# Final norm of the last token half: squares summed by a matrix of ones, the root by ScalarE and a Newton step on rows, other tiles for GpSimd

## The chip, the cores and the metric

The kernel runs on one core of a Trainium2 chip. The core has five engines that work beside each other, each through its own queue in order: TensorE (PE: matrix products; PEld is its loading of the stationary operand), VectorE (DVE), ScalarE (ACT), GpSimd (POOL) and SyncE (SP, which here only issues transfers). The metric is the device time of one execution in microseconds (us); less is better.

## What is computed

One layer of a hybrid decoder over 512 tokens of width 2048, and then a last RMSNorm. The change concerns only the last line:

```python
def rmsnorm(x, w):
    xf = x.astype(jnp.float32)
    y = xf * lax.rsqrt(jnp.mean(xf * xf, axis=-1, keepdims=True) + EPS)
    return (y * w.astype(jnp.float32)).astype(x.dtype)

...
        x = x + conv_ffn(rmsnorm(x, norm2_w[l]), ffn_up[l], ffn_conv_w[l], ffn_down[l])
    return rmsnorm(x, final_norm_w)
```

Each token's 2048 values are divided by the root of their mean square and multiplied by a weight for each of the 2048 features.

## The kernel before

**Layout.** Activations lie transposed: 128 features on the partitions, tokens along the row. The 2048 features are 16 tiles `acc[0]` to `acc[15]` of 128x512; two neighbours share a buffer `acc2[d // 2]`. In the profile the buffer appears as `accd`. Because features lie on partitions, a token's sum of squares runs over partitions and over the 16 tiles, and needs TensorE.

**The last stretch.** The down projection of the feed-forward part adds its products into `acc` chunk by chunk. The last chunk of both weight halves is treated apart, and in two token halves `t` = 0 and 1 of 256 tokens (`HS`), so that the norm of half 0 can run beside the products of half 1. For each tile `d` of a half (function `parts`): six products into a PSUM tile `ps_e` (L201 to L203: float32 values split into a high and a low part), VectorE adds it to `acc[d]` (L1089), ScalarE squares the result (L1095 for d = 0, straight into the running sum `s3`; L1097 into `sq` for the others), and GpSimd adds the square to `s3` (L1099). The last `NP[t]` squares (2 in half 0, 6 in half 1) aren't added by GpSimd but go to TensorE.

**The norm of a half** (generator `finish`, L1039 to L1056). ScalarE multiplies the tiles that GpSimd is to scale, d >= `ND_` = 10, by their norm weight (L1042, "prescale" below). TensorE then sums squares over the partitions (`sums`, L1034): each square is the stationary operand, in two pieces of 128 tokens, and a single column of ones is the moving one; so the sums stand as 128x2, token on partition. VectorE takes the mean and the inverse root by an integer guess and three Newton steps, twelve operations on 128x2 (L1048 and L130 to L135). TensorE turns the result back into a row of 256 tokens on all partitions, in PSUM (L118, tile `n_ps`), and ScalarE copies it to SBUF (L1055, `r3`; the profile calls it `rstd`).

**Scaling** (`scale`). For d < 10, VectorE multiplies `acc[d]` by the norm weight and by the row in PSUM (L1063). For the other six, GpSimd multiplies the prescaled tile by the copy `r3` (L1066). After each odd tile SP issues the transfer of the pair to the output `outT` (L1068).

**Order.** In this stretch the order on TensorE, SP, VectorE, ScalarE and GpSimd is that in which the program issues the instructions; a small clock `self.now`, moved by estimates, decides when a waiting generator such as `finish` goes on between products. The scaling of half 0 is issued between the tiles of half 1: behind tile d > `AFTER` = 9 of half 1 stand the scalings of tiles d - 10 and, on GpSimd, d. All tiles of half 1 are scaled at the end, after the last product.

Of the kernel before, what the change touches and what calls it, by code (L numbers as in the profile page):

```python
# [8 lines left out]
F32 = mybir.dt.float32  # L9
# [3 lines left out]
AF = mybir.ActivationFunctionType  # L13
ALU = mybir.AluOpType
# [4 lines left out]
P = 128  # L19
S = 512  # L20
D = 2048
KT = D // P
# [6 lines left out]
EPS = 1e-6  # L29
# [50 lines left out]
class Body:  # L80
# [704 lines left out]
    def out_phase(self):  # L785
        tc, nc, io = self.tc, self.nc, self.io
        with ExitStack() as ctx:
            pool = lambda name, **k: ctx.enter_context(tc.tile_pool(name=name, **k))
            g2 = pool("g2", bufs=1)
# [227 lines left out]
            j0 = NFF - G  # L1017
            wl = [wd[c - 1], wd[c]]
            HS = S // 2
            NP, ND_ = (2, 6), 10  # L1020
            s3 = g2.tile([P, 2, HS], F32, tag="ssum", name="ssum3")
            r3 = g2.tile([P, 2, HS], F32, tag="rstd", name="rstd3")

            pts, norm_row, sq4 = {}, {}, {}
            AFTER = 9

            def sums(t, parts, last=False):

                first = t not in pts
                if first:  # L1030
                    pts[t] = self.mm.tile([P, S], F32, tag="mm", name=f"ps_n3_{t}")
                for i, q in enumerate(parts):
                    for c in range(HS // P):
                        nc.tensor.matmul(pts[t][:, c:c + 1], q[:, c * P:(c + 1) * P], self.ones[:, 0:1],  # L1034
                                         start=first and i == 0 and c == 0, stop=last and i == len(parts) - 1,
                                         skip_group_check=True)
                        self.now += 0.21

            def finish(t, late):  # L1039
                sl = slice(t * HS, (t + 1) * HS)  # L1040
                for d in range(ND_, KT):
                    nc.scalar.activation(acc[d][:, sl], acc[d][:, sl], AF.Copy, scale=self.prm("nf", d))  # L1042
                yield 4.0 if t == 0 else 0.5
                n = HS // P
                sums(t, late[-2:] + [s3[:, t, :]], last=True)
                pt = pts[t]
# [8 lines left out]
                nc.scalar.copy(out=r3[:, t, :], in_=ps[:, 0:HS])  # L1055
                norm_row[t] = ps  # L1056

            def scale(t, e):

                sl = slice(t * HS, (t + 1) * HS)  # L1060
                a = acc[e][:, sl]
                if e < ND_:
                    nc.vector.scalar_tensor_tensor(out=a, in0=a, scalar=self.prm("nf", e), in1=norm_row[t][:, 0:HS],  # L1063
                                                   op0=ALU.mult, op1=ALU.mult)
                else:
                    nc.gpsimd.tensor_tensor(out=a, in0=a, in1=r3[:, t, :], op=ALU.mult)  # L1066
                if e % 2:
                    nc.sync.dma_start(out=io["outT"][:, e - 1:e + 1, sl], in_=acc2[e // 2][:, :, sl])  # L1068

            for t in range(2):  # L1070
                sl = slice(t * HS, (t + 1) * HS)
# [8 lines left out]
                def parts(ds):  # L1080
# [4 lines left out]
                    for d in ds:  # L1085
# [12 lines left out]
                        if d < KT - NP[t]:  # L1098
                            nc.gpsimd.tensor_tensor(out=s3[:, t, :], in0=s3[:, t, :], in1=q, op=ALU.add)  # L1099
                        else:  # L1100
                            late.append(q)
                            if len(late) > 2:
                                sums(t, late[-3:-2])
                        if t == 1 and d > AFTER:
                            self.ensure(lambda: 0 in norm_row)
                            scale(0, d - AFTER - 1)
                            if d - AFTER - 1 + ND_ < KT:
                                scale(0, d - AFTER - 1 + ND_)

                if n8:  # L1110
                    parts(range(n8))
                for d in range(n8, KT):
                    parts([d])
                if t == 1:
                    for e in range(KT - AFTER - 1, ND_):
                        scale(0, e)
                self.spawn(finish(t, late))
            self.ensure(lambda: not self.cos)
            for e in (0, 1, 10, 2, 3, 11, 4, 5, 12, 6, 7, 13, 8, 9, 14, 15):
                scale(1, e)  # L1120


class UpProjection:
# [191 lines left out]
```

## Time and profile before

| | |
|---|---|
| median of 3 runs | 2228.73 us (2227.31 to 2229.14) |
| profiled execution, its own time | 2227.93 us |
| its span in the trace | 2226.2 us |
| TensorE busy | 2198.1 us, 99% of the span |
| VectorE busy | 1519.4 us, 68% |
| ScalarE busy | 947.7 us, 43% |
| GpSimd busy | 426.1 us, 19% |
| granted TensorE clock, mean | 0.995 of full speed |

A row of the timeline gives start, duration, engine, line of the program, operation, output <- inputs, shape and count, and in brackets how long the engine had been idle before it and what ended that. Rows that are merged ("x5") overlap a little at their seams. Times are from the start of the span. A group of the costliest instructions shows busy time in us, mean duration in ns, and idle time before them.

### The profile page before, as it was taken

Reading aid. Unit: us, or ns where it says so; the run is one execution under the profiler, and the core shown is the slowest. Engines: PE = TensorE matmul, PEld = TensorE weight load, DVE = VectorE, ACT = ScalarE, POOL = GpSimd, SP = SyncE. Lnnn points to the kernel's source line nnn. Section 1 sums busy time; section 2 is a strip of 40 time slices with the busy share of each in tenths; the row PEclk is TensorE's granted clock in tenths of the full one; section 3 lists DMA queues with packets and bytes.
Section 4 is the critical chain, followed back from the end, with each engine's and each line's share of the span. In section 5 each row is a group of like instructions: output and inputs, shape, how many; then the busy total and the mean of one; then the engine's idle time right before and its main releaser. Section 6 shows DMA issues by size and latency. Waiting matters only on the chain.

```text
span 2226.2 us, 35449 instructions
## 1 busy us (share of the span) xinstructions
PE 2198.1 (99%) x13998; PEld 1990.0 (89%) x13998; DVE 1519.4 (68%) x2346; ACT 947.7 (43%) x1377; POOL 426.1 (19%) x519
## 2 busy tenths in 40 slices
PE   8999999999999999999999999999999999999997
PEld 6888888888888999999999999999998888888887
DVE  7766667665445776766676666677667777777776
ACT  6656455434334544444444444444443222222223
POOL 5270811800121211111111111111110000000004
PEclk9999999999999999999999999999999999999998
DMA  6232232323534788888888888888885333333342
GB/s 199 77 111 67 79 102 83 100 66 119 193 118 137 168 204 196 206 207 200 201 196 198 206 203 199 202 196 201 219 192 188 130 125 116 123 114 123 114 129 99
DMA packets 109207, 340.01 MB, mean 153 GB/s; under 512 B 12720, under 2 KB 19120, under 8 KB 109040
## 3 DMA queue, kind: packets, MB, share of 16 engines
q1 hardware_dynamic: 78576, 229.72, 30.2%
q0 software_dynamic: 30464, 108.02, 26.6%
q8 instruction: 110, 1.80, 0.3%
q14 instruction: 57, 0.47, 0.1%
HBM read 314.36 MB, written 23.33 MB: 152 GB/s over the span
## 4 chain that ended last, share of the span: by engine, by line
PE 90%; DVE 3%; POOL 3%; issue 2%; DMA 1%; ACT 1%; SPq 0%; POOLq 0%; ACTq 0%; DVEq 0%
PE ps_y L1193 18%; PE ps_x L1193 12%; PE ps_z L1193 12%; PE ps_d L203 8%; PE ps_d L201 7%; PE ps_d L202 7%; PE ps_u L201 4%; PE ps_u L202 4%; PE ps_u L203 4%; PE ps_o L202 3%; PE ps_o L201 3%; PE ps_o L203 3%; POOL tl L583 1%; POOL tm L581 1%; PE ps_x L118 1%
## 5 line engine op out<-in xcount | busy, mean ns | idle before, releaser
L1010 DVE TENSOR_TENSOR accd<-accd,ps_d 128x512 f32<-128x512 f32 x368 | 250.0, 685 | 125.3 <-PE ps_d L203 125.3
L201 PE MATMUL ps_d<-gh,whi_d 128*128 128x512 f32 x736 | 286.3, 389 | 0.0
L202 PE MATMUL ps_d<-gl,whi_d 128*128 128x512 f32 x736 | 286.3, 389 | 0.0
L203 PE MATMUL ps_d<-gh,wlo_d 128*128 128x512 f32 x736 | 286.3, 389 | 0.0
L1193 PE MATMUL ps_y<-fs,hi_t 128*128 128x256 f32 x1536 | 269.7, 278 | 2.6 <-ACT hi_b L1174 1.3
L274 ACT CAST whi_d<-raw_d 128x1024 fp32r<-128x1024 f32 x96 | 100.8, 1053 | 370.8 <-PE ps_d L202 346.9
L1175 DVE TENSOR_TENSOR lo_t<-ra,hi_t 128x1024 fp32r<-128x1024 f32 x144 | 176.0, 1223 | 114.3 <-ACT hi_t L1174 114.2
L201 PE MATMUL ps_u<-xh,hi_in 128*128 128x512 f32 x608 | 245.7, 404 | 0.0
L203 PE MATMUL ps_u<-xh,lo_in 128*128 128x512 f32 x608 | 237.9, 391 | 0.0
L202 PE MATMUL ps_u<-xl,hi_in 128*128 128x512 f32 x608 | 237.4, 391 | 0.0
L1193 PEld LDWEIGHTS ps_y<-fs,hi_t 128*128 128x128 f32 x1536 | 232.9, 188 | 3.0 <-ACT e L1215 1.5
L1178 POOL DMA_DIRECT2D ra<-in_w_up x144 | 126.2, 876 | 555.3 <-DVE lo_t L1175 455.9
L1193 PE MATMUL ps_y<-fs,lo_t 128*128 128x256 f32 x768 | 213.1, 277 | 0.0
L1174 ACT CAST hi_t<-ra 128x1024 fp32r<-128x1024 f32 x144 | 151.3, 1051 | 72.7 <-PE ps_y L1193 44.7
L202 PEld LDWEIGHTS ps_d<-gl,whi_d 128*128 128x128 f32 x736 | 138.2, 188 | 28.7
L203 PEld LDWEIGHTS ps_d<-gh,wlo_d 128*128 128x128 f32 x736 | 138.2, 188 | 28.6
L201 PEld LDWEIGHTS ps_d<-gh,whi_d 128*128 128x128 f32 x736 | 138.2, 188 | 28.5
L1193 PEld LDWEIGHTS ps_y<-fs,lo_t 128*128 128x128 f32 x768 | 144.4, 188 | 0.0
L1193 PE MATMUL ps_y<-fb,hi_t 128*128 128x256 f32 x768 | 140.1, 283 | 1.2 <-DVE e L1223 1.2
L1193 PE MATMUL ps_x<-fb,hi_b 128*128 128x256 f32 x768 | 140.1, 283 | 0.0
L1193 PE MATMUL ps_x<-fa,hi_b 128*128 128x256 f32 x768 | 140.0, 283 | 0.0
L203 PEld LDWEIGHTS ps_u<-xh,lo_in 128*128 128x128 f32 x608 | 114.2, 188 | 24.8
(357 smaller groups left out, 5087.8 us busy)
## 6 DMA issues: line engine op xcount, KB each, us to landing
ra<-in_w_up POOLq DMA_DIRECT2D x144, 512.0 KB, 7.8
raw_d<-in_w_down SPq DMA_DIRECT2D x96, 512.0 KB, 4.2
raw_in<-in_w_in SPq DMA_DIRECT2D x80, 512.0 KB, 3.7
ra<-in_w_up SPq DMA_DIRECT2D x48, 512.0 KB, 7.0
rc<-in_w_up SPq DMA_DIRECT2D x48, 512.0 KB, 6.6
rb<-in_w_up SPq DMA_DIRECT2D x48, 512.0 KB, 7.3
rb<-in_w_up POOLq DMA_DIRECT2D x48, 512.0 KB, 7.4
raw_o<-in_w_out SPq DMA_DIRECT2D x32, 512.0 KB, 3.7
```

The source lines that it names most:

```text
L118: self.nc.tensor.matmul(out, lhsT, rhs, start=True, stop=True)
L201: nc.tensor.matmul(ps, hi[:, sl], a, start=start, stop=False)
L202: nc.tensor.matmul(ps, hi[:, sl], b, start=False, stop=False)
L203: nc.tensor.matmul(ps, lo[:, sl], a, start=False, stop=stop)
L274: self.nc.scalar.copy(out=hi, in_=x)
L581: nc.gpsimd.tensor_tensor(out=t, in0=bc(ll[:, j, j + 1:32], j + 1), in1=tl[:, j:j + 1, 0:j + 1].broadcast_to([32, m, j + 1]), op=ALU.mult)
L583: nc.gpsimd.tensor_tensor(out=tl[:, j + 1:32, 0:j + 1], in0=tl[:, j + 1:32, 0:j + 1], in1=t, op=ALU.subtract)
L1010: nc.vector.tensor_tensor(out=acc[d], in0=acc[d], in1=ps, op=ALU.add)
L1174: nc.scalar.copy(out=hi, in_=raw)
L1175: nc.vector.tensor_tensor(out=lo, in0=raw, in1=hi.bitcast(F32), op=ALU.subtract)
L1178: nc.gpsimd.dma_start(out=raw, in_=self.block(j, self.NEXT[f]), accum_op=ALU.add)
L1193: mm = lambda w, x, s, e: nc.tensor.matmul(ps, w[:, sl], x, start=s, stop=e, skip_group_check=True)
```

## The change

For half 1, each square (and the running sum `s3`) is now the moving operand of one product with a 128x128 matrix of ones; the sum of a token then stands on all partitions at once, as a row of 256 tokens. ScalarE takes the square root of that row, and VectorE makes the inverse root by a reciprocal and one Newton step on 128x256; the result goes to `r3` in SBUF, and that is the row for both engines' scaling. Half 0 keeps the old way. The one use of the square root earlier, on a single value, stands where its table is loaded. GpSimd scales tiles 8 to 15 of half 0 and tiles 4 to 9 of half 1 (before: 10 to 15 of both); the prescales of half 1 stand behind the square of the same tile. Of half 1, tiles 0 and 1 are sent one by one.

```diff
-            NP, ND_ = (2, 6), 10
+            NP = (2, 6)
+            ON_POOL = range(8, 16), range(4, 10)
...
+            eps = g2.tile([P, 2], F32, name="eps")
+            nc.vector.memset(eps, EPS)
+            nc.scalar.activation(eps[:, 1:2], eps[:, 0:1], AF.Sqrt)
...
+                if t == 1:
+                    for i, q in enumerate(parts):
+                        nc.tensor.matmul(pts[t][:, 0:HS], self.ones, q, start=first and i == 0,
+                                         stop=last and i == len(parts) - 1)
+                        self.now += 0.43
+                    return
...
+            def prescale(t, ds):
+                sl = slice(t * HS, (t + 1) * HS)
+                for d in ds:
+                    nc.scalar.activation(acc[d][:, sl], acc[d][:, sl], AF.Copy, scale=self.prm("nf", d))
+
             def finish(t, late):
-                sl = slice(t * HS, (t + 1) * HS)
-                for d in range(ND_, KT):
-                    nc.scalar.activation(acc[d][:, sl], acc[d][:, sl], AF.Copy, scale=self.prm("nf", d))
-                yield 4.0 if t == 0 else 0.5
+                if t == 1:
+                    yield 0.5
+                    sums(t, late[-2:], last=True)
+                    tt, row = nc.vector.tensor_tensor, pts[t][:, 0:HS]
+                    ms, y, u = (ep.tile([P, HS], F32, tag=f"ea{2 + i}", name=f"n3_{k}")
+                                for i, k in enumerate(("ms", "y", "u")))
+                    nc.scalar.activation(u, row, AF.Sqrt, scale=1.0 / D, bias=eps[:, 0:1])
+                    nc.vector.tensor_scalar(ms, row, 1.0 / D, EPS, op0=ALU.mult, op1=ALU.add)
+                    nc.vector.reciprocal(y, u)
+                    nc.vector.scalar_tensor_tensor(out=u, in0=y, scalar=-0.5, in1=y, op0=ALU.mult, op1=ALU.mult)
+                    tt(out=u, in0=u, in1=ms, op=ALU.mult)
+                    nc.vector.scalar_tensor_tensor(out=r3[:, t, :], in0=u, scalar=1.5, in1=y, op0=ALU.add, op1=ALU.mult)
+                    norm_row[t] = r3[:, t, :]
+                    return
+                prescale(t, ON_POOL[t])
+                yield 4.0
...
-            def scale(t, e):
+            def scale(t, e, alone=False):
...
-                if e < ND_:
+                if e not in ON_POOL[t]:
...
-                if e % 2:
-                    nc.sync.dma_start(out=io["outT"][:, e - 1:e + 1, sl], in_=acc2[e // 2][:, :, sl])
+                if alone or e % 2:
+                    n = 1 if alone else 2
+                    nc.sync.dma_start(out=io["outT"][:, e + 1 - n:e + 1, sl],
+                                      in_=acc2[e // 2][:, e % 2 + 1 - n:e % 2 + 1, sl])
...
+                        if t == 1 and d == KT - 1:
+                            sums(t, [s3[:, t, :]])
+                        if t == 1 and d in ON_POOL[t]:
+                            prescale(t, [d])
                         if t == 1 and d > AFTER:
                             self.ensure(lambda: 0 in norm_row)
                             scale(0, d - AFTER - 1)
-                            if d - AFTER - 1 + ND_ < KT:
-                                scale(0, d - AFTER - 1 + ND_)
+                            scale(0, d - AFTER - 1 + 8)
...
-                    for e in range(KT - AFTER - 1, ND_):
+                    for e in range(KT - AFTER - 1, 8):
                         scale(0, e)
+                        scale(0, e + 8)
...
-            for e in (0, 1, 10, 2, 3, 11, 4, 5, 12, 6, 7, 13, 8, 9, 14, 15):
-                scale(1, e)
+            for e in (0, 1, 4, 5, 2, 3, 10, 11, 6, 7, 12, 13, 8, 9, 14, 15):
+                scale(1, e, alone=e < 2)
```

What this does to the order on ScalarE, from the square of d = 6 of half 1 on. Names carry the tile: `accd6` holds d = 6 and 7, `sq3_1_4` the squares of d = 4 to 7 of half 1, `rstd3` is `r3`, `n3_ps0` the row of half 0. Before:

```order
L1097 ACTIVATE sq3_1_4_21445<-accd6_17289 128x256 x2
L1097 ACTIVATE sq3_1_8_21509<-accd8_17383 128x256 x2
L1097 ACTIVATE sq3_1_8_21509<-accd10_17455 128x256
L1055 COPY rstd3_21229<-n3_ps0_21531 128x256
L1097 ACTIVATE sq3_1_8_21509<-accd10_17455 128x256
L1097 ACTIVATE sq3_1_12_21558<-accd12_16630 128x256 x2
L1097 ACTIVATE sq3_1_12_21558<-accd14_16665 128x256 x2
L1042 ACTIVATE accd10_17455<-accd10_17455,prmt_77 128x256 x2
```

With the change, from the same square on:

```order
L1126 ACTIVATE sq3_1_4_21450<-accd6_17289 128x256
L1052 ACTIVATE accd6_17289<-accd6_17289,prmt_77 128x256
L1126 ACTIVATE sq3_1_4_21450<-accd6_17289 128x256
L1052 ACTIVATE accd6_17289<-accd6_17289,prmt_77 128x256
L1126 ACTIVATE sq3_1_8_21518<-accd8_17383 128x256
L1052 ACTIVATE accd8_17383<-accd8_17383,prmt_77 128x256
L1126 ACTIVATE sq3_1_8_21518<-accd8_17383 128x256
L1052 ACTIVATE accd8_17383<-accd8_17383,prmt_77 128x256
L1126 ACTIVATE sq3_1_8_21518<-accd10_17455 128x256
L1082 COPY rstd3_21229<-n3_ps0_21542 128x256
L1126 ACTIVATE sq3_1_8_21518<-accd10_17455 128x256
```

Four prescales (L1052) now stand between the square of d = 6 and the copy of half 0's row, where there were none; before, prescales of half 1 (L1042) came after all squares.

On VectorE, the end of the program before (the last scalings of half 0, the norm of half 1, its first scaling; most rows of the Newton steps are left out at the dots):

```order
L1063 SCALAR_TENSOR_TENSOR accd8_17383<-accd8_17383,prmt_77,n3_ps0_21531 128x256 x2
L1048 TENSOR_SCALAR ms3_1_21626<-ps_n3_1_21560 128x2
L130 TENSOR_SCALAR n3_1_t_21630<-ms3_1_21626 128x2
L131 TENSOR_SCALAR n3_1_y_21629<-n3_1_t_21630 128x2
L133 SCALAR_TENSOR_TENSOR n3_1_t_21630<-n3_1_y_21629 128x2
...
L135 SCALAR_TENSOR_TENSOR rt3_1_21628<-n3_1_t_21630,n3_1_y_21629 128x2
L1063 SCALAR_TENSOR_TENSOR accd0_17480<-accd0_17480,prmt_77,n3_ps1_21642 128x256 x2
```

And with the change:

```order
L1090 SCALAR_TENSOR_TENSOR accd6_17289<-accd6_17289,prmt_77,n3_ps0_21542 128x256 x2
L1062 TENSOR_SCALAR n3_ms_21624<-ps_n3_1_21571 128x256
L1063 RECIPROCAL n3_y_21625<-n3_u_21626 128x256
L1064 SCALAR_TENSOR_TENSOR n3_u_21626<-n3_y_21625 128x256
L1065 TENSOR_TENSOR n3_u_21626<-n3_u_21626,n3_ms_21624 128x256
L1066 SCALAR_TENSOR_TENSOR rstd3_21229<-n3_u_21626,n3_y_21625 128x256
L1090 SCALAR_TENSOR_TENSOR accd0_17480<-accd0_17480,prmt_77,rstd3_21229 128x256 x2
```

Twelve operations on 128x2 became five on 128x256, and the scaling of half 1 reads its row from `rstd3` in SBUF, where before it read `n3_ps1` in PSUM.

## The prediction

> **What bounds the kernel now.** I read first the chain of work that ended last, then the timeline of its last 25 us engine by engine, then the windows of the output transfers. By line and engine the chain is
>
> ```profile
> PE 90%; DVE 3%; POOL 3%; issue 2%; DMA 1%; ACT 1%; SPq 0%; POOLq 0%; ACTq 0%; DVEq 0%
> ```
>
> TensorE bounds the run, but the change leaves its products as they are. It touches only what follows them: the final norm of token half 1, and the place where half 0's norm ends. So the sum is made there. The timeline of VectorE (start, duration, idle before and what ended it):
>
> ```profile
> 2200.80 0.58 DVE L133 SCALAR_TENSOR_TENSOR n_t<-n_y 128x2 f32<-128x2 f32 x1
> 2202.23 0.16 DVE L133 SCALAR_TENSOR_TENSOR n_t<-n_y 128x2 f32<-128x2 f32 x1
> 2203.29 1.74 DVE L1089 TENSOR_TENSOR accd<-accd,ps_e 128x256 f32<-128x256 f32 x5
> 2205.77 0.48 DVE L1063 SCALAR_TENSOR_TENSOR accd<-accd,prmt,n_ps 128x256 f32<-128x256 f32 x1 [0.75 <-ACT rstd L1055]
> 2209.71 0.42 DVE L1089 TENSOR_TENSOR accd<-accd,ps_e 128x256 f32<-128x256 f32 x1 [0.35 <-PE ps_e L203]
> 2212.07 0.16 DVE L1048 TENSOR_SCALAR ms<-ps_n 128x2 f32<-128x2 f32 x1
> 2214.24 0.16 DVE L135 SCALAR_TENSOR_TENSOR rt<-n_t,n_y 128x2 f32<-128x2 f32 x1
> 2216.12 4.00 DVE L1063 SCALAR_TENSOR_TENSOR accd<-accd,prmt,n_ps 128x256 f32<-128x256 f32 x10 [1.72 <-ACT rstd L1055]
> ```
>
> The first scaling of half 0 (2205.77) waits for ScalarE's copy L1055 and not for the row itself. The last addition of half 1 (d=15) starts at 2209.71, the first scaling of half 1 at 2216.12: 6.41 us in which the norm is made. ScalarE, TensorE and GpSimd beside it:
>
> ```profile
> 2182.95 1.05 ACT L274 CAST whi_d<-raw_d 128x1024 fp32r<-128x1024 f32 x1
> 2186.39 0.42 ACT L1095 ACTIVATE ssum<-accd 128x256 f32<-128x256 f32 x1 [2.39 <-DVE accd L1089]
> 2195.00 2.49 ACT L1042 ACTIVATE accd<-accd,prmt 128x256 f32<-128x256 f32 x6
> 2203.74 1.74 ACT L1097 ACTIVATE sq<-accd 128x256 f32<-128x256 f32 x5 [4.32 <-DVE accd L1089]
> 2205.38 0.35 ACT L1055 COPY rstd<-n_ps 128x256 f32<-128x256 f32 x1
> 2210.16 0.42 ACT L1097 ACTIVATE sq<-accd 128x256 f32<-128x256 f32 x1 [0.74 <-DVE accd L1089]
> 2203.43 0.71 PE L118 MATMUL n_ps<-cst,rt 128*128 128x128 f32 x4
> 2203.89 0.36 PE L201 MATMUL ps_e<-gh,whi_d 128*128 128x256 f32 x1
> 2208.71 0.36 PE L201 MATMUL ps_e<-gh,whi_d 128*128 128x256 f32 x1
> 2209.39 0.28 PE L203 MATMUL ps_e<-gh,wlo_d 128*128 128x256 f32 x1
> 2209.51 0.95 PE L1034 MATMUL ps_n<-cst,sq 128*128 128x1 f32 x8
> 2198.18 4.00 POOL L1099 TENSOR_TENSOR ssum<-ssum,sq 128x256 f32<-128x256 f32 x5 [0.35 <-ACT sq L1097]
> 2216.16 4.14 POOL L1066 TENSOR_TENSOR accd<-accd,rstd 128x256 f32<-128x256 f32 x6 [4.54 <-ACT rstd L1055]
> ```
>
> In the scaling of half 1 VectorE (10 tiles, 4.00 us) and GpSimd (6 tiles, 4.14 us) run side by side. Then the output transfers: their first issue, and windows (columns: busy us and count of PE, PEld, DVE, ACT, POOL; granted clock; DMA share; GB/s):
>
> ```profile
> 2217.02 0.37 SPq L1068 DMA_DIRECT2D outT<-accd  x1
> 2217.00:2218.00 1.00, 0.00 (x0) 0.00 (x0) 1.00 (x3) 0.00 (x0) 1.00 (x2) 0.50 0.06 23
> 2218.00:2219.00 1.00, 0.00 (x0) 0.00 (x0) 1.00 (x4) 0.00 (x0) 1.00 (x3) 0.50 1.02 331
> 2223.00:2224.00 1.00, 0.00 (x0) 0.00 (x0) 0.00 (x0) 0.00 (x0) 0.00 (x0) 0.50 1.04 353
> 2224.00:2225.00 1.00, 0.00 (x0) 0.00 (x0) 0.00 (x0) 0.00 (x0) 0.00 (x0) 0.50 0.13 38
> ```
>
> Bytes move from about 2217.95, 0.93 us after the first issue, without a gap to about 2224.1. Eight pairs of 256 KB in 6.2 us are 0.77 us each. The span ends at 2226.2, 2.1 us later. So today's end is the first issue (0.90 us after the first scaling) plus 0.93 plus 6.2 plus 2.1: scaling is faster than the transfers need.
>
> **Part 1: prescales move ahead of the copy (+2.6 us at the copy, +2.7 at the last addition).** Before, ScalarE's six multiplications by the norm weight for half 1 came after all squares. Now one stands behind each square of d = 4 to 9, and the copy of half 0's row still stands behind the square of d = 10. A square takes 0.42 us, and 0.33 from start to start where it waits for nothing (the row of five); a prescale 0.41 from start to start (the row of six). A prescale waits for the square of its own tile (a wait costs some 0.04, as from addition 15, done at 2210.13, to its square at 2210.16), so a pair takes 0.42 + 0.04 + 0.41 = 0.87. Four pairs and one square are 3.8 us instead of 1.64 (2205.38 - 2203.74): +2.2. Also, two more prescales of half 0 (0.83 us) push half 1's first squares back, and GpSimd's five sums of 2198.18 end near 2203.0 instead of 2202.2. VectorE's small Newton ops on two SBUF operands are held there: 0.58 us beside GpSimd, 0.16 after. One more sum in that chain costs 0 to 0.8; I take 0.4, half of one 0.80 us sum. The copy then ends near 2208.35, and VectorE's queue is in order: behind the waiting scaling stand the additions 11 to 15, and for their squares waits TensorE. So: scaling 2208.4, addition 11 at 2208.8, its square done at 2209.7, its product with ones 0.43, main products of d=14 0.80 (2208.71 to 2209.51), ones 0.43, main products of d=15 0.96 to their result (2208.71 to 2209.67), addition 15 at 2212.4, against 2209.71. The place that the prescales leave (after the squares) was idle time of ScalarE and gains nothing.
>
> **Part 2: the row form of the norm (-0.7 us).** From addition to square 0.92 as before. The 128x256 product with ones has no row; its columns are those of the two 128x128 products of L118, which hold the engine 0.46 us (2203.43 to 2203.89) and give their result after 0.71. Bounds 0.4 and 0.95 (the eight at 2209.51); I take 0.43 and 0.59 to a result. At d=15 four are queued (13, the running sum, 14, 15), and the last ends 1.68 after addition 15 starts. Then Sqrt from PSUM: the copy takes 0.35, a prescale with a pointer scale 0.49 in the mean of the groups below; 0.46, and 0.04 to wait. The row form on VectorE:
>
> ```profile
> L149 DVE RECIPROCAL spg_s<-spg_s 128x24 f32<-128x24 f32 x1 | 0.3, 286 | 0.0
> L149 DVE RECIPROCAL spl_s<-spl_s 128x6 f32<-128x6 f32 x1 | 0.2, 192 | 0.0
> L1042 ACT ACTIVATE accd<-accd,prmt 128x256 f32<-128x256 f32 x12 | 5.0, 493 | 0.0
> L737 ACT ACT_TABLE_LOAD x6 | 7.7, 1283 | 0.1
> ```
>
> The reciprocal of 256 columns has no row. The two small ones differ by 94 ns for 18 columns, 5.2 ns a column: an estimate of 1.5 us. Ends: 0.42 (a plain 128x256 op) and 3.05 (286 ns / 24 x 256). The other four are plain: ms 0.44 with its wait, two of 0.52, one of 0.46. From addition 15 to the first scaling: 1.68 + 0.50 + 0.44 + 1.50 + 1.50 + 0.04 = 5.66, against 6.41. The twelve small ops (2212.07 to 2214.40), the broadcast and the copy go; what is late next is the reciprocal. The first op, ms, waits for Sqrt although it reads the same row; behind it stand the whole norm and all scaling. The three scalings of half 0 ahead of it (five before) end near 2214.0, before Sqrt does, so moving two of them to GpSimd gains nothing, and its eight tiles of half 0 (0.69 each, from 2208.4) end near 2213.9, before half 1's row is there. The first scaling comes at 2218.05, 1.93 later than now.
>
> The table load for Sqrt stands once, behind the last weight cast at 2184.0; ScalarE is idle there until 2186.39, which hides its 1.28 us. Without that cover it would cost 1.28. The memset (one small op) lies in VectorE's idle time there: nothing.
>
> **Part 3: scaling of half 1 (+1.8 us).** Before, VectorE's row operand lay in PSUM. Now it is r3 in SBUF, so both operands lie in SBUF while GpSimd reads there. What that does stands at the other end of the run:
>
> ```profile
> L239 DVE SCALAR_TENSOR_TENSOR xl<-xraw,n,xh x16: 740/1762/1786, 5.3 to 37.6; 128x512 fp32r<-128x512 f32 x16
> 12.53 8.58 DVE L239 SCALAR_TENSOR_TENSOR xl<-xraw,n,xh 128x512 fp32r<-128x512 f32 x5
> 12.16 17.96 POOL L227 TENSOR_TENSOR ssum<-ssum,sq 128x512 f32<-128x512 f32 x10 [0.64 <-ACT sq L226]
> ```
>
> The same op takes 0.74 us at its shortest and 1.76 in the median; beside it GpSimd does one op in 1.80. The two take turns, one each in 1.72 to 1.80 us. Half the width is half of it: 0.90 a turn. GpSimd's six tiles then last 5.4 us with six of VectorE's, and the other four follow at 0.40: the last tile is ready 6.6 after the first scaling starts. The first transfer leaves earlier (one tile alone, 0.5), but the stream breaks: tiles 10 and 11 go out at +5.05, their bytes from +5.98, then five pairs at 0.77, then 2.1: end at +11.9. Today it is +10.08 (2226.2 - 2216.12). SP issues nine transfers for half 1 and not eight, at 0.37 each, never back to back: nothing. With nothing shared: 0.5 + 0.93 + 6.2 + 2.1 and 0.2 of gaps, +9.9. One after the other: VectorE's 4.0 and GpSimd's 4.14 make 8.1 us, +13.1. I take the turns, since the row is of the same two ops.
>
> The Trainium skill, "SBUF — State Buffer", section "Who interferes with whom", speaks against this edit: a VectorE instruction with two SBUF inputs contends with a GpSimd instruction that reads SBUF, and the pair of ports is "an exclusive lock". The trace agrees that they hold each other up; by a lock held for whole instructions the sum would be 1.2 us more, while the turn of 1.80 us is shorter than that.
>
> **The sum.** 1.93 + 1.8 = +3.7 us on the profiled run: 2227.93 (its span 2226.2 and 1.73 around it) becomes 2231.6. That run lies 0.80 below the median of 2228.73; on the median it is 2232.4. About 0.2% (4.5 us) is what a measurement of this kernel can tell from no change, so the forecast is a loss too small to tell.
>
> **Rivals.**
>
> Side by side (0.15): half 1's scaling is not held up, as between 2216.16 and 2220.30 today. For it: none of today's scalings show contention; against: their row is in PSUM. 1.93 - 0.2 = +1.7: 2230.4.
>
> A small gain (0.08): besides that, the prescales cost nothing, because the square of d=10 and the copy find a free ScalarE. For it: ScalarE idles 4.32 us before 2203.74; against: the additions come in one burst at 2203.29, so the squares are queued. -0.7 - 0.2 = -0.9: 2227.8.
>
> The clock falls (0.17): TensorE now waits from the end of d=12's products (near 2205.8) to the square of d=10 (near 2208), where it never waited over 0.2 us in half 1. In the run before, the granted clock fell close to the end:
>
> ```profile
> 2210.00:2211.00 1.00, 0.82 (x9) 0.74 (x8) 1.00 (x4) 0.83 (x3) 1.00 (x3) 1.00 1.02 336
> 2211.00:2212.00 1.00, 1.00 (x7) 0.94 (x6) 1.00 (x3) 1.00 (x3) 0.62 (x1) 0.59 1.03 346
> ```
>
> If it falls in the new wait, the 2.6 us of products from 11's square to addition 15 and four products with ones run at half speed: +2.6 to +4.5 on top of 3.7 if it stays, +1.2 if half of them are hit, so 2233.6 to 2236.9. It decides once the clock reads under 1 between 2206 and 2212. Against it: the 256-column products keep the engine busier than 128x1 ones. The Trainium skill, "TensorE: Matmul & The Clock Gate", Part 1, lets the clock fall after an idle window of about 3.4 us, which a wait of 2.2 would not fill; the trace shows a fall with no such idle time, so the chance stays.
>
> Not what it says (0.05): the square or copy set lacks Sqrt, and a load returns at the end: +1.28, 2233.7.
>
> **How the numbers follow.** Forecast 0.55, from 2231 to 2234 with the reciprocal's ends; about a fifth of that lies above 2233.2. Slower by over 0.2%: 0.11 + 0.17 + 0.04 = 0.32; faster by over 0.2%: 0.02; within: 0.66. The range leaves out the small gain and the tip of the clock's case: 2228.8 to 2236.2.
>
> **What would show it.** The copy L1082 ending 2 to 3 us later against the additions; TensorE idle before the product of d=10's square; the reciprocal at 1.5 us; scalings of half 1 at 0.8 to 0.9 us while GpSimd works and 0.4 after; breaks in the output stream. Wrong if those scalings stay at 0.40 beside GpSimd, or the copy does not move.

## The result, and the profile after

The changed kernel takes **2247.02 us** in the median of 4 runs (2245.81 to 2248.63), the kernel before, beside it, 2228.70 (2227.31 to 2229.14): ratio 1.0088, 95% interval 1.0076 to 1.0100. It is slower by 18.3 us. The forecast was 2232.4 in a range that ended at 2236.2, so it was wrong, and by more than any rival allowed. One execution of a later run (the ninth of e6) took 7810.78 us, over three times as long as its ten others; it stands in no ratio, and its cause is open.

The last stretch, of which the prediction made its sum, did what it said. VectorE's timeline of after (start, duration, idle before and what ended it; a choice of rows, answering to the rows of before):

```profile
2214.54 0.58 DVE L133 SCALAR_TENSOR_TENSOR n_t<-n_y 128x2 f32<-128x2 f32 x1
2216.18 0.59 DVE L134 TENSOR_TENSOR n_t<-n_t,ms 128x2 f32<-128x2 f32 x1
2217.46 1.74 DVE L1118 TENSOR_TENSOR accd<-accd,ps_e 128x256 f32<-128x256 f32 x5
2222.01 0.48 DVE L1090 SCALAR_TENSOR_TENSOR accd<-accd,prmt,n_ps 128x256 f32<-128x256 f32 x1 [2.81 <-ACT rstd L1082]
2225.91 0.42 DVE L1118 TENSOR_TENSOR accd<-accd,ps_e 128x256 f32<-128x256 f32 x1 [0.33 <-PE ps_e L203]
2228.55 1.74 DVE L1063 RECIPROCAL n_y<-n_u 128x256 f32<-128x256 f32 x1
2230.40 0.42 DVE L1064 SCALAR_TENSOR_TENSOR n_u<-n_y 128x256 f32<-128x256 f32 x1
2231.78 6.95 DVE L1090 SCALAR_TENSOR_TENSOR accd<-accd,prmt,rstd 128x256 f32<-128x256 f32 x10
```

The chain that ended last, by engine, reads as before (TensorE 89% and not 90):

```profile
PE 89%; DVE 4%; POOL 2%; ACT 2%; issue 1%; DMA 1%; SPq 0%; DVEq 0%; ACTq 0%; POOLq 0%
```

All of the last stretch stands some 14 us later than forecast, and so does its beginning. The first product of the last stretch, from TensorE's timeline of before and then of after:

```profile
2182.50 0.28 PE L201 MATMUL ps_e<-gh,whi_d 128*128 128x256 f32 x1
```

```profile
2196.26 0.28 PE L201 MATMUL ps_e<-gh,whi_d 128*128 128x256 f32 x1
```

Of the 17.6 us between the two spans (2243.8 and 2226.2), 13.76 have come about before any changed instruction runs. Behind that point the stretch takes 2243.8 - 2196.26 = 47.5 us against 43.7: +3.8, where +3.7 was forecast.

The 13.8 us lie in the up projection, of which the change touches no line: its first product starts at 731.0 us in before and 730.2 in after, its last at 1681.9 and 1695.6. There TensorE runs back-to-back products of 256 columns, in threes for each of eight blocks `kt`: high weights by high and by low activations, low weights by high activations. These 24 products, into one PSUM tile, are called a column block below. The moving operands are `fa` and `fb` (split blocks of the input, in pool acts), and `fs` (sums of blocks; `kt` 0 to 5 in pool ffn, 6 and 7 in acts). A pool is a stretch of SBUF, the memory that holds these operands, from which tiles are taken; the pools lie one behind the other. Windows of 200 us (busy us and number of recorded products, granted clock, DMA share, GB/s), before, then after:

```profile
800.00:1000.00 200.00, 200.00 (x1710) 1.00 0.86 201
1000.00:1200.00 200.00, 200.00 (x1710) 1.00 0.85 202
```

```profile
800.00:1000.00 200.00, 200.00 (x1683) 1.00 0.85 198
1000.00:1200.00 200.00, 200.00 (x1683) 1.00 0.85 198
```

1.6% fewer products in the same time, at a granted clock of 1.00 and without a gap: of some 950 us that is 15. The groups of TensorE's instructions say which products (the last number ahead of the idle time is the mean ns of one; the line moved from L1193 to L1226). Before, then after:

```profile
L1193 PE MATMUL ps_z<-fs,hi_b 128*128 128x256 f32 x768 | 134.9, 278 | 0.0
L1193 PE MATMUL ps_x<-fa,hi_b 128*128 128x256 f32 x768 | 140.0, 283 | 0.0
```

```profile
L1226 PE MATMUL ps_z<-fs,hi_b 128*128 128x256 f32 x768 | 138.5, 282 | 0.0
L1226 PE MATMUL ps_x<-fa,hi_b 128*128 128x256 f32 x768 | 140.3, 283 | 0.0
```

Products overlap, so the pitch (start to start) is what counts. The first product of `kt` 0 and that of `kt` 6 of one column block are 18 products apart; before, then after:

```profile
1001.48 0.40 PE L1193 MATMUL ps_y<-fs,hi_t 128*128 128x256 f32 x2
1003.54 0.39 PE L1193 MATMUL ps_y<-fs,hi_t 128*128 128x256 f32 x2
```

```profile
1010.48 0.40 PE L1226 MATMUL ps_y<-fs,hi_t 128*128 128x256 f32 x2
1012.60 0.40 PE L1226 MATMUL ps_y<-fs,hi_t 128*128 128x256 f32 x2
```

2.06 us are 114.4 ns a product, 2.12 are 117.8, to the 0.5 that rows of 0.01 us allow. In the median of all 188 column blocks of `fs` that run into the next without a pause it is 114.4 and 118.2 for `kt` 0 to 5, and about 117.8 and 118.8 for `kt` 6 and 7; `fa` and `fb` have 119.8 and 120.0. So nearly all of the loss is at products that read `fs`, and what the change did to `fs` is to move it. The tile `eps` takes 32 bytes of a partition in pool g2, and pool ffn lies behind g2: in the built programs every tile of ffn starts 32 bytes higher (`fs` of block 0 at byte 180160 in place of 180128), while weights (32480 and on) and pool acts (65248 and on) stay.

### The profile page after: what moved, and what is told of

Its sections match the earlier page's. It is cut to its first block, busy times and chain, and to the rows that moved or that the text cites. A ratio compares the mean times of both kernels' runs of the same rounds, so it can differ in the third digit from the quotient of the medians.

```text
span 2243.8 us, 35418 instructions
## 1 busy us (share of the span) xinstructions
PE 2211.5 (99%) x13980; PEld 2003.0 (89%) x13980; DVE 1523.1 (68%) x2338; ACT 949.4 (42%) x1381; POOL 425.8 (19%) x521
## 4 chain that ended last, share of the span: by engine, by line
PE 89%; DVE 4%; POOL 2%; ACT 2%; issue 1%; DMA 1%; SPq 0%; DVEq 0%; ACTq 0%; POOLq 0%
PE ps_y L1226 18%; PE ps_x L1226 12%; PE ps_z L1226 12%; PE ps_d L201 7%; PE ps_d L202 7%; PE ps_d L203 7%; PE ps_u L201 4%; PE ps_u L202 4%; PE ps_u L203 4%; PE ps_o L201 3%; PE ps_o L203 3%; PE ps_o L202 3%; POOL tl L583 1%; POOL tm L581 1%; DVE lo_in L189 1%
## 5 line engine op out<-in xcount | busy, mean ns | idle before, releaser
L1226 PE MATMUL ps_y<-fs,hi_t 128*128 128x256 f32 x1536 | 276.9, 282 | 1.8 <-DVE e L1252 1.8
L1226 PEld LDWEIGHTS ps_y<-fs,hi_t 128*128 128x128 f32 x1536 | 235.4, 189 | 2.2 <-ACT e L1248 1.2
L1226 PE MATMUL ps_y<-fs,lo_t 128*128 128x256 f32 x768 | 214.9, 280 | 0.0
L1226 PEld LDWEIGHTS ps_y<-fs,lo_t 128*128 128x128 f32 x768 | 145.6, 190 | 0.0
L1226 PE MATMUL ps_y<-fb,hi_t 128*128 128x256 f32 x768 | 140.4, 283 | 1.2 <-DVE e L1256 1.2
L1226 PE MATMUL ps_x<-fb,hi_b 128*128 128x256 f32 x768 | 140.3, 283 | 0.0
L1226 PE MATMUL ps_x<-fa,hi_b 128*128 128x256 f32 x768 | 140.3, 283 | 0.0
L1226 PE MATMUL ps_z<-fs,hi_b 128*128 128x256 f32 x768 | 138.5, 282 | 0.0
```

The source lines that it names most:

```text
L1226: mm = lambda w, x, s, e: nc.tensor.matmul(ps, w[:, sl], x, start=s, stop=e, skip_group_check=True)
```

## The experiments

"Distance" below is the start of the moving operand minus the start of the weights, modulo 256 bytes: 192 for `fs` in ffn before and 224 after, 0 for everything in acts. Where a time stands beside "before", it is that of the kernel before on the same chip in the same series.

**e1: the 32 bytes alone.** The kernel before and

```diff
+            pad = g2.tile([P, 8], F32, name="pad")
+            nc.vector.memset(pad, 0.0)
```

> The kernel before with nothing but a tile of 8 elements (32 bytes a partition) taken from pool g2 and cleared once: every tile of pool ffn moves up by 32 bytes, as the tile eps moves it in the change. Theory address: the products that read fs from pool ffn fall from 113 ns to about 117-118 ns each, and the run takes 2228.7 + 13.8 = 2242.5 us (2239 to 2246). Rival rest-of-change: the new instructions of the last stretch, or their wiring, cost the time; then this kernel stays at 2228.7 us (within 2).

2241.50 us (2239.30 to 2242.89), before 2227.84; ratio 1.0059 (1.0046 to 1.0073): +13.7 us with no other edit. The group that stood at 278 ns reads as in the changed kernel:

```profile
L1195 PE MATMUL ps_z<-fs,hi_b 128*128 128x256 f32 x768 | 138.5, 282 | 0.0
```

**e2: the whole change without the 32 bytes.** The changed kernel and

```diff
-                rt = g2.tile([P, n], F32, tag=f"rt{n}", name=f"rt3_{t}", bufs=2)
+                rt = g2.tile([P, n], F32, tag=f"rt{n}", name=f"rt3_{t}", bufs=1)
```

> The changed kernel with the second buffer of the small tile rt3 given up (only one is in use), so that eps takes its 32 bytes and every other tile lies where it lay before the change. Theory address: the 13.8 us before the last stretch come back and only the last stretch's own cost stays: 2247.0 - 13.8 = 2233.2 us (2231 to 2235); the prediction on record had 2232.4. Rival rest-of-change: it stays near 2247 us.

2233.76 us (2229.60 to 2234.42), ratio 1.0022 (1.0014 to 1.0031): +3 to +7 us on before. e1 and e2 tell the theories apart from two sides: the address costs 13.7 us, the last stretch the rest. In the profiled execution one rival of the prediction came true as well. Windows of TensorE (busy, products, granted clock, DMA share, GB/s):

```profile
2207.73:2209.73 2.00, 0.49 (x2) 0.92 0.00 0
2209.73:2211.73 2.00, 2.00 (x9) 0.50 0.04 13
2211.73:2213.73 2.00, 2.00 (x11) 0.73 0.90 303
```

TensorE waits for the squares, the clock falls to 0.50, and the stretch takes 2232.4 - 2183.73 = 48.7 us in place of 47.5: the +1.2 that the rival gave if half of the products are hit. In the profiled run of after the clock held in the same wait (1.00 in every window from 2207 to 2229 us). The eleven executions of e2 stand in two groups: seven from 2233.6 to 2234.4 us with a mean granted clock of 0.993 or 0.994, the profiled one among them, and four from 2229.6 to 2231.2 with 0.995 or 0.996. So the fall is likely in the seven; that it alone makes the 3 us between the groups is not shown.

**e3 and e4: place or distance?** First a table without the rest of the kernel:

```python
for i in range(n):
    nc.tensor.matmul(ps[:, 0:width], wt[:, wo + P * (i % 4):wo + P * (i % 4) + P],
                     mv[:, mo + HT * (i % 3):mo + HT * (i % 3) + width], start=i == 0, stop=i == n - 1)
```

> All of the computation is left out; only products of zeros and of one tile of x are run, with the start of the moving operand at each of eight places (a to h: 0, 32, ... 224 bytes modulo 256) and the start of the weights at four (a to d: 0, 32, 64, 96 modulo 128), 96 products of 256 columns each (ps_h) and 48 of 512 columns for two places of the weights (ps_f). Theory address, absolute: with 256 columns the pitch is about 113 ns where the moving operand starts at 32 modulo 128 (b, f), 118 at 64 (c, g), 120 at 96 (d, h), whatever the weights' place; 0 (a, e) is unknown. Theory address, relative to the weights: with the weights at 96 (d) the same, and with the weights at another place the fast place moves along with them. Rival traffic: no place differs by over 1 ns, since nothing else reads or writes here. Whether 512 columns show the same gap of some 6 ns is open.

With 256 columns the pitches went from 113.3 to 119.9 ns with no other engine at work, so rival traffic falls. The slow and fast places moved along with the weights: 119.8 to 119.9 at distance 0 for all four places of the weights, and 113.6 at 192 for three of them (117.8 for the fourth; one place of distance 64 had 113.3 besides, which stayed unexplained). 512 columns went the other way: 227.1 ns at distance 0, 229 at 64, about 233 at the others.

In the same series, the kernel before with 64 bytes ahead of pool acts:

```diff
+            pad = pool("pad", bufs=1).tile([P, 16], F32, name="pad")
+            nc.vector.memset(pad, 0.0)
             self.ap_ = pool("acts", bufs=1)
```

> The kernel before with 64 bytes a partition put ahead of pool acts: the moving operands of pool acts start at 32 modulo 128 in place of 96, those of pool ffn at 96 in place of 32; the weights stay. Theory address: the 4608 products of 256 columns on acts tiles in the up projection go from 120 to 113.5 ns (-30 us), the 3456 on ffn tiles from 113.5 to 120 (+22 us): about 2221 us if products of 512 columns are not touched; if the 4800 products of 512 columns gain the same 6.5 ns each, some 31 us less again, about 2190 us. Rival traffic or rest-of-change: 2228.7 us, within 2.

2244.85 us (2244.80 to 2245.43), ratio 1.0075 (1.0060 to 1.0091): slower, a miss for the absolute place. By distance it comes out: `fs` in ffn is now at 0 (120.2 ns in the median of its column blocks, +5.8 for 3456 products), `fa` and `fb` at 64 (117.8, -2.0 for 3456), and the products of 512 columns at 64 (228.7 in place of 227.1 in the table below, some 4900 of them): an estimate of +20.0 - 6.9 + 7.8 = +21 us, measured +17. From its first to its last product the up projection takes 12.9 us more in the trace, near the 13.1 of the first two terms; the excess is in the third.

**e8: everything up by 32 bytes**, so that places change and distances don't.

```diff
+            pad = cp.tile([P, 8], F32, name="pad")
+            nc.vector.memset(pad, 0.0)
             self.prmt = cp.tile([P, NPRM], F32, name="prmt")
```

> The kernel before with a 32-byte tile at the front of pool const: weights, activations and pool ffn all move up by 32 bytes together, so that their distances stay and only the absolute places change. Theory distance (the pitch goes by where the moving operand starts relative to the weights): the fs products of pool ffn keep 114 ns and the time stays at 2227.8 us, within 2.5. Theory place (the pitch goes by the moving operand's own place modulo 128): fs at 64 modulo 128 as in the change, 118 ns, about 2241.5 us.

2226.93 us (2224.62 to 2230.80), before 2226.07, ratio 1.0003 (0.9994 to 1.0012); `fs` at 114.4 ns. It is the distance and not the place.

**e9: a table with the kernel's own addresses and order.** Weights in two tiles and two moving operands in threes, as in the kernel, the moving ones shifted by 32 bytes from letter to letter (`one` and `two` lie as tiles of acts do, `far` as those of ffn; in `oneq` and `onez` the weights lie 128 and 384 bytes further).

> All of the computation is left out; only products of zeros, with weights and moving operands at the addresses and in the order of the kernel (two tiles of weights, two moving operands, in threes), the moving operand shifted by 0 to 480 bytes in steps of 32 (a to p). one: 256 columns as fa; two: 512 columns; far: 256 columns as fs of pool ffn; oneq, onez: as one with the weights 128 and 384 bytes further. Theory distance: one shows 120 ns at a (as in the kernel), about 118 at c (as fa in e4), 113 to 114 at g (the distance of fs before); far 114 at a, 118 at b, 120 at c; oneq is one moved on by 4 letters and onez by 12; the pattern repeats after 8 letters (256 bytes). two: 227 at a, 229 at c, about 233 at the others. Theory place: oneq and onez equal one, letter by letter. Rival other-engines: all letters alike within 1 ns, and the kernel's differences come from what DMA and the other engines do beside it.

Timeline (the pitch is the gap to the next group's start by the count):

```profile
61.48 5.92 PE L282 MATMUL ps_one_a<-ma,wt 128*128 128x256 f32 x48
67.24 11.07 PE L282 MATMUL ps_two_a<-ma,wt 128*128 128x512 f32 x48
78.14 3.70 PE L282 MATMUL ps_far_a<-mf,wt 128*128 128x256 f32 x30
...
183.58 5.61 PE L282 MATMUL ps_one_g<-ma,wt 128*128 128x256 f32 x48
189.03 11.36 PE L282 MATMUL ps_two_g<-ma,wt 128*128 128x512 f32 x48
200.22 3.72 PE L282 MATMUL ps_far_g<-mf,wt 128*128 128x256 f32 x30
203.78 5.84 PE L282 MATMUL ps_one_h<-ma,wt 128*128 128x256 f32 x48
209.46 11.36 PE L282 MATMUL ps_two_h<-ma,wt 128*128 128x512 f32 x48
...
409.59 5.62 PE L282 MATMUL ps_oneq_c<-ma,wt 128*128 128x256 f32 x48
415.05 5.60 PE L282 MATMUL ps_onez_c<-ma,wt 128*128 128x256 f32 x48
```

(67.24 - 61.48) / 48 = 120.0 ns at distance 0, 5.45 / 48 = 113.5 at 192 (g), 5.68 / 48 = 118.3 at 224 (h). The first is `fa`, the second is `fs` before, the third `fs` after. Worked out in this way for all letters:

| distance, bytes | 0 | 32 | 64 | 96 | 128 | 160 | 192 | 224 |
|---|---|---|---|---|---|---|---|---|
| 256 columns, ns | 120.0 | 116.7 | 117.9 | 120.0 | 118.5 | 117.3 | 113.5 | 118.3 |
| 512 columns, ns | 227.1 | 233.3 | 228.7 | 233.3 | 232.5 | 234.4 | 233.1 | 233.3 |

The letters i to p repeat a to h within 0.3 ns, and with the weights 128 bytes further the fast place moves from g to c (5.46 / 48 = 113.8): distance again. One row misses: `far`, at 192 in its first letter, has (81.68 - 78.14) / 30 = 118.0 ns, and 117.7 at the same distance eight letters on, where the kernel before has 114.4. The distance alone doesn't fix the pace at 192; e10 to e13 come back to this.

**e5, e6 and e7: the parts of the last stretch**, on e2. e5 takes the prescales from between the squares:

```diff
-                        if t == 1 and d in ON_POOL[t]:
-                            prescale(t, [d])
...
                     nc.scalar.activation(u, row, AF.Sqrt, scale=1.0 / D, bias=eps[:, 0:1])
+                    prescale(t, ON_POOL[t])
```

> The changed kernel with the addresses of before (as e2) and the six prescales of the second half put behind the Sqrt of the row form in place of between the squares. Theory of the prediction (part 1): four prescales ahead of the copy that frees the first half's scalings hold it and, behind it, addition 15 by 2.7 us; without them the run ends 2.7 us before e2 (2233.8), at 2231.1 (2230 to 2232.3); in the trace addition 15 comes 2.7 us sooner after the start of the last stretch. Rival: the copy is held by the Newton step, which waits for GpSimd's hold of VectorE, and not by the prescales; then under 1 us is gained (2232.8 or more).

e6 gives VectorE its row in PSUM; e7 has both edits:

```diff
-                    nc.vector.scalar_tensor_tensor(out=r3[:, t, :], in0=u, scalar=1.5, in1=y, op0=ALU.add, op1=ALU.mult)
-                    norm_row[t] = r3[:, t, :]
+                    ps = self.aux.tile([P, S], F32, tag="aux", name=f"n3_ps{t}")
+                    nc.vector.scalar_tensor_tensor(out=ps[:, 0:HS], in0=u, scalar=1.5, in1=y, op0=ALU.add, op1=ALU.mult)
+                    nc.scalar.copy(out=r3[:, t, :], in_=ps[:, 0:HS])
+                    norm_row[t] = ps
```

> The changed kernel with the addresses of before (as e2), the last Newton instruction of the second half writing its row to PSUM, from where ScalarE copies it to SBUF for GpSimd (0.35 us) and VectorE scales out of PSUM, as it did before the change. Theory of the prediction (part 3): VectorE's scalings with both operands in SBUF take turns with GpSimd's; from PSUM they run beside them, and the run ends 1.8 us less 0.35 us for the copy sooner than e2 (2233.8): about 2232.3 (2231.5 to 2233). In the trace VectorE's 10 scalings take near 0.45 us each where GpSimd runs, in place of 0.70. Rival: where the row lies does not matter, the tile itself is in SBUF in both; then 2233.8 to 2234.2.

> e5 and e6 together: addresses of before, prescales of the second half behind the Sqrt, the norm row in PSUM for VectorE. Theory: the parts add up; from the start of the last stretch to the end of the span e2 took 48.7 us, e5 44.9 and e6 46.7, so 43.0 here, 0.7 us less than the 43.7 of before: the row form's own gain, and a time within 0.1% of before. Rival: the prescales behind the Sqrt run beside the scalings and take part of e6's gain away: 43.7 or more, and a time of before or slower.

VectorE's scalings of half 1 in e2 and then in e6:

```profile
2220.44 6.94 DVE L1090 SCALAR_TENSOR_TENSOR accd<-accd,prmt,rstd 128x256 f32<-128x256 f32 x10
```

```profile
2218.76 4.01 DVE L1092 SCALAR_TENSOR_TENSOR accd<-accd,prmt,n_ps 128x256 f32<-128x256 f32 x10 [0.44 <-ACT rstd L1068]
```

us from the first product of the last stretch, each from its own trace:

| | addition 15 | first scaling of half 1 | end | ratio of times to before (95%) |
|---|---|---|---|---|
| before | 27.2 | 33.6 | 43.7 | 1 |
| after | 29.7 | 35.5 | 47.5 | 1.0088 (1.0076 to 1.0100) |
| e2: addresses of before | 30.9 | 36.7 | 48.7 | 1.0022 (1.0014 to 1.0031) |
| e5: e2, prescales late | 27.6 | 33.5 | 44.9 | 1.0007 (0.9999 to 1.0016) |
| e6: e2, row in PSUM | 30.8 | 37.1 | 46.7 | 1.0020 (1.0011 to 1.0030) |
| e7: both | 27.6 | 33.9 | 43.5 | 1.0000 (0.9991 to 1.0009) |

e5: 3.3 us up to addition 15, where 2.7 were expected. In the trace of e5 the granted clock stays at 1.00 in this part, where it fell in e2, which is part of the 3.3. e6, in whose trace the clock fell as in e2: scalings of 4.01 us in place of 6.94, and 2.0 us at the end, near the 1.45 expected; the timing alone doesn't resolve it. The medians, 2228.08 us for e5 and 2231.30 for e6, lie under the ranges expected; the kernel before had 2226.07 in this series and 2227.84 in that of e2. e7: the parts add up to 43.5 (43.0 expected), with a median of 2227.51 us beside 2226.98. Without its two costs the change is no measurable gain either: from addition 15 to the first scaling the row form takes 6.28 us in e7 against 6.41 before, since the copy for GpSimd now holds VectorE for 0.44.

**e10 and e11: can the fast distance be had for all?** e10 is the kernel before with the up projection's weights 64 bytes further in their slots (and small tiles moved so that the rest fits), so that 512 columns keep distance 0 and all of the up projection has 192; e11 is e10 with e7's last stretch.

```diff
+            self.wbig = self.wp.tile([P, 8 * 1024 + 16], F32R, tag="wbig", name="wbig")
...
+        o = self.wshift + 1024 * k
+        return self.wbig[:, o:o + 1024], self.wbig[:, o + 1024 * NW:o + 1024 * NW + 1024]
...
-            hi = wp.tile([P, 1024], F32R, tag="whi", name=f"hi_{f}_{j}", bufs=NW)
-            lo = wp.tile([P, 1024], F32R, tag="wlo", name=f"lo_{f}_{j}", bufs=NW)
+            self.b.wshift = 16
+            hi, lo = self.b.wpair()
```

> The kernel before with weights and activations at other distances and nothing else: the eight weight slots are one tile with 64 bytes to spare, and the up projection's weights start 64 bytes further in it than those of the other stages; pool small moves behind pool wts and the small tiles of the norms move into it, so that acts and ffn both start at the distance 0 modulo 256 from the other stages' weights (as acts did) and 192 modulo 256 from the up projection's (as ffn did). Theory distance, from the second table (letters a, g): the 3456 products on fa and fb go from 120 to 113.5 ns (-22 us), the 1152 on fs in acts from 116 to 120 down to 113.5 (-4 us), the rest stays: about 2200 us (2195 to 2206); if the fs of ffn fall to the 118 ns that far showed at this distance, 12 us more. Rival: the up projection's pace is set beside TensorE by its transfers or by VectorE (85% and 70% busy there); then fa and fb stay near 120 ns, or wait in pauses, and the time stays near 2226.

> e10 and e7 together: the distances of e10 with the changed last stretch of e7. Theory: both gains add up, about 0.7 us under e10, near 2199 us. Rival: if either theory falls, as e10 or e7 falls.

Neither: e10 had a median of 2231.13 us, e11 of 2231.15, before 2226.98, and the 24 runs of the two fell apart: five from 2200.3 to 2208.7, one at 2223.1, eighteen from 2229.5 to 2233.9. e10's ratio of 0.9999 (0.9971 to 1.0027) is a mean over two cases. The profiled run of e11 shows the step from one to the other (windows of TensorE):

```profile
1340.00:1360.00 20.00, 20.00 (x179) 1.00 0.87 198
1360.00:1380.00 20.00, 20.00 (x172) 1.00 0.89 210
1380.00:1400.00 20.00, 20.00 (x173) 1.00 0.84 200
```

Up to about 1360 us it records 179 products in 20 us, then 172 to the end of the stage, at the same clock. One distance has two paces. The kernel before holds one: in all 188 column blocks of `fs` in its trace that run into the next without a pause, `kt` 0 to 5 have 114 ns; its very last one, behind a pause, has 118 up to `kt` 6. It also has, in each such block, six products at distance 0 (`kt` 6 and 7), which e10 has not.

**e12 and e13: products at another distance in between.** e10 (its small tiles packed closer, which makes room), with the `fs` tiles of `kt` 5 (e12), or of 4 and 5 (e13), moved 64 bytes, to distance 0:

```diff
+                if p == 5:
+                    pad = ep.tile([P, 16], F32, name="pad")
+                    nc.vector.memset(pad, 0.0)
                 if p < HK - 2:
```

> As e10 (the up projection's weights 64 bytes further, acts and ffn at the distance 192 from them), but the two fs tiles of the sixth block pair (p=5) lie 64 bytes further, at the distance 0: in each of the four fs products of a column block, 3 of 24 products run at 120 ns. Theory two paces: at the distance 192 the products run at 113 ns until something disturbs them, and then at 118 until products at another distance have come between; the kernel before has such products in every fs product, and all its 157 fs products that were read ran at 114; e10 has none. Then here nearly all of the rest runs at 113 to 114 in every execution: against before 576 x 120 + 7488 x 114 in place of 3456 x 120 + 3456 x 114.4 + 1152 x 116.2 ns, 21 us less, near 2206 us (2201 to 2212), with no execution near 2231. Rival: the pace is set once for an execution or drawn anew, whatever lies between; then it scatters between 2201 and 2233 as e10 did.

> As e12, with the fs tiles of the fifth and the sixth block pair at the distance 0: 6 of 24 products, as many as lie at that distance in every fs product of before. Theory two paces, if 3 products are enough to bring the fast pace back: 1152 x 120 + 6912 x 114 ns, 18 us less than before, near 2209 us, 3 above e12. If it takes 6: e12 scatters, and this kernel does not. Rival as for e12.

e12: **2202.46 us** (2200.76 to 2208.58), before 2228.12, ratio 0.9891 (0.9876 to 0.9906). e13: 2205.66 (2203.69 to 2207.24), 0.9900 (0.9883 to 0.9916). None of the eight runs is near 2231, and e13 is 3.2 above e12 (3 expected). Windows of e12:

```profile
800.00:1000.00 200.00, 200.00 (x1760) 1.00 0.87 207
1000.00:1200.00 200.00, 200.00 (x1760) 1.00 0.88 209
```

1760 products in place of 1710 before and 1683 after, with DMA moving 207 GB/s in place of 201: the transfers did not set the pace. e12 beats the kernel before by 1.1%, and so the changed one too, without an edit to the work of the last stretch.

The trace of e12 also shows the pace fall and come back (rows of TensorE; `wbig` holds the weights):

```profile
1594.13 3.07 PE L1206 MATMUL ps_y<-fs,wbig 128*128 128x256 f32 x24 [0.26 <-DVE e L1232]
1597.04 2.98 PE L1206 MATMUL ps_z<-fs,wbig 128*128 128x256 f32 x24
1599.86 2.88 PE L1206 MATMUL ps_y<-fb,wbig 128*128 128x256 f32 x24
1602.58 2.90 PE L1206 MATMUL ps_z<-fs,wbig 128*128 128x256 f32 x24
```

From start to start, the block behind the pause takes 2.91 us, the next 2.82 (117.5 ns a product), and the `fb` block 2.72 (113.3). Product by product the pace stays at about 118 ns through the first block's three products at distance 0 and is back at 113 behind those of the second. A pause is not all there is to it: in e10's trace the pace changed behind several pauses near 750 us, once back to 113 ns as well, and stayed at 118 from 758 us on; e11's step stands at a block start at 1360.84 us before which no wait is recorded.

## Why the prediction was wrong

**The step that failed** stands in its first part: "TensorE bounds the run, but the change leaves its products as they are." The instructions are the same and in the same order; their operands are not in the same place. `eps`, costed at "nothing" as one small op, moves pool ffn by 32 bytes, and 3456 `fs` products go from 114.4 to 118.2 ns: 3456 x 3.8 = 13.1 us. The products beside them, at distance 0 in both kernels, add a little (1152 x 1.0 at `kt` 6 and 7, 3456 x 0.2 for `fa` and `fb`: 1.8). That is 14.9 us; from its first to its last product the up projection takes 14.5 more, and it starts 0.7 earlier. e1 shows that this is enough, e2 that without it the change costs +3 to +7 us, e8 that the distance from the weights decides. The prediction read the order of the instructions and not the addresses, and no rival had its place outside the last stretch. The sum for the last stretch, +3.7, was right in its mechanisms, with small errors that cancel by luck: part 1 measured 0.3 us less than forecast, parts 2 and 3 0.2 and 0.1 more.

**Part 1** held. The copy ended 2.45 us later in the stretch than before (25.7 against 23.2; 2.6 forecast), addition 15 started 2.4 later (2.7 forecast), three and not two Newton operations were held by GpSimd, and in e5, without the prescales in between, addition 15 is back at 27.6 us (27.2 before). There the copy ends at 23.6, so the prescales are 2.1 of the delay (2.2 forecast) and the rest of the chain 0.4, as forecast.

**Part 2** held, with a size off: the reciprocal of 256 columns took 1.85 us to the next start, not 1.5. From addition 15 to the first scaling came 5.87 us (5.66 forecast, 6.41 before). The table load lay in ScalarE's idle time as said.

**Part 3** held. From the first scaling to the end came 12.0 us (11.9 forecast, 10.1 before); the ten scalings took 6.95 (6.6 forecast). A turn of one scaling on each engine took 0.94 us (0.90 forecast), less than the two alone, one after the other, would (0.47 and 0.69). e6 shows that it is where the row lies: 4.01 us out of PSUM. The Trainium skill, "SBUF — State Buffer", "Who interferes with whom", says that a VectorE instruction with two SBUF inputs contends with a GpSimd instruction that reads SBUF, and that one with at most one SBUF input, outside some faster modes, does not; by that, the same tiles beside the same GpSimd work run free once one input is in PSUM, and the trace of e6 agrees.

**The rivals.** Side by side, a small gain and a table load at the end are ruled out by the trace of after. The falling clock came in the profiled runs of e2, at the price given, +1.2 us, and of e6, and not in those of after, e5 and e7; by the granted clocks of its executions it is likely in seven of e2's eleven, so the chance of 0.17 was probably low.

**Still open.** Why the pitch goes by the distance: no run here looks inside. The Trainium skill, "SBUF — State Buffer", "A bandwidth-pool intuition that's wrong", gives the loading of weights a read port of its own; by that alone, the place of the weights would not matter to the moving operand, and here it does (113.5 to 120.0 ns), so a port of its own is not all there is to it. Also open: what throws the products at distance 192 into the slow pace, and why other products bring the fast one back; that they do rests on 8 runs against 24 and on the place in e12's trace shown above.

## What to carry to other kernels

Where TensorE runs products back to back, a new tile of a few bytes can be an edit to all that lies behind it: compare the addresses of the operands of the longest stage before and after, and allocate small tiles last or into free slots. Read the pitch, start to start, of the same products by tile: two pitches for one shape in one stage (114 and 120 ns here) may be a gain to be had by moving a buffer, as e12 was. And when a time differs from the sum, look first at where in the run the traces part, before looking at the edited lines.

## What the runs showed of the hardware

- The pitch of a 128x256 float32 product in back-to-back work went from 113.5 to 120.0 ns (table of e9) with the distance between moving operand and weights modulo 256 bytes, that of a 128x512 one from 227.1 to 234.4; the distance that is best for one width (192 and 0) is not best for the other.
- At distance 192 there are two paces, 113 to 114 and about 118 ns; two kernels whose up projection is all at this distance scattered by over 30 us between executions, and three products in 24 at distance 0, in the column blocks of `fs` alone, kept it near the fast end in all four runs taken.
- The Trainium skill, "TensorE: Matmul & The Clock Gate", "Wait — 56ns, not 53.3ns?", has a fixed addition of about 2.5 ns to the columns at full clock, an estimate of 109 ns for 256 columns; no pitch of 256 float32 columns worked out here lies below 113.3.
